# Row sums of squares for the first norm: a second load of x with its sums on ScalarE, in place of GpSimd additions

## The chip, the cores and the metric

One core of a Trainium2 chip runs the whole program. The metric is device time in microseconds (us), median of three runs. Engines: TensorE (PE in the profile; its weight loads are PEld), VectorE (DVE), ScalarE (ACT), GpSimd (POOL), and SyncE (SP), from whose queue nearly all DMA transfers are issued.

## The reference

A hybrid decoder layer on x of 512 tokens by 2048 columns, float32:

```python
h = _rmsnorm(x, norm_w[l])              # x * rsqrt(mean(x*x over the 2048 columns) + 1e-6) * norm_w
p = h @ w_in[l]                         # 2048 x 7824
y_a = _rwkv7_mix(...)                   # RWKV-7 time mixing, 16 heads of 64
y_b = _moba_mix(...)                    # block attention, 4 heads of 128
y_c = _gla_mix(...)                     # gated linear attention, 4 heads of 128
x = x + jnp.concatenate([y_a, y_b, y_c], axis=-1) @ w_out[l]
return _rmsnorm(x, final_norm_w)
```

The norm's factor per token, rsqrt(mean(x*x) + eps), commutes with the product by w_in. The kernel multiplies x by norm_w and by w_in first and applies the factor to the product. So the sums of squares are not needed for the first products, but for whatever reads them.

## The kernel before, in words

**Products.** w_in is computed in 62 jobs of 128 columns, in the order of `ORDER` (lines 40 to 42): wdad, k0, ga0, ga1, r0, k1, low, v0, r1, v1, gk0, gq0 and so on. A job is four units (`low` is a single one of 16 columns); a unit is one load of 128x512 of w_in and its products: four blocks of 128 rows, and for each three matmuls of 128x512, as each operand is split into a float32r high part and the rest (`hhi`, `hlo` for x, `hi`, `lo` for the weights). A unit is thus 12 matmuls. The first three jobs run side by side, since the transposed x arrives only then: units 0 to 11 are wdad, k0, ga0 for the first quarter of x's columns, then for the second, and so on. Units 12 to 15 are ga1, 16 to 19 r0, 20 to 23 k1, 24 low, 25 to 28 v0, 29 to 32 r1, 33 to 36 v1, 37 to 40 gk0, 41 to 44 gq0.

**Buffers.** A unit is loaded into one of three `raw` buffers (the load waits until the split of the unit three before it is done), split by ScalarE (`hi`, line 173) and VectorE (`lo`, line 133) into one of four pairs `hi`, `lo`. So the split of unit u waits for TensorE's last product of unit u-4, and `begin(u)` issues the splits up to unit u+3 ahead of everything else that unit u needs.

**Banks.** A job adds up in one of four PSUM banks `gb`, taken in turn: a job takes the bank of the job four before it and must wait until that one is evacuated (`evac`, line 340: VectorE multiplies it by `rstd_b`, the factor of each token). `job_bank` (line 180) calls `wait_free` for that, and `force` (line 303) then emits whatever work is left up to the evacuation. 62 jobs make 58 such hand-overs.

**Side work** (the mixers) is written as generators that `pump` (line 295) resumes between the products. When, a rough clock model of the queues decides (`Clock`, line 62). The result is a fixed order of instructions on each engine; the engines take their queues strictly in that order.

**The statistics** are such side work: `square` (line 1093) squares each of the 16 transposed tiles of x on ScalarE into `f1` to `f3`, GpSimd adds them into `f0` (line 1103), and `stats` (line 365) sums `f0` over the partitions by four matmuls against a column of ones (line 116), copies the result to `rst`, scales it (line 149), takes the power -1/2 on GpSimd (line 362), spreads it by four transposes (line 125) and copies it to `rstd_b` (line 153). Every evacuation waits for `rstd_b`.

Of the kernel before, what the change touches and what calls it, by code (L numbers as in the profile page):

```python
# [25 lines left out]
# first columns of the parts of w_in  # L26
# [4 lines left out]
# columns of the per-partition parameters  # L31
P_NW, P_MU, P_W0, P_A0, P_KK, P_KA, P_RK, P_LW, P_LB, P_GB, P_GN = 0, 16, 41, 49, 57, 65, 73, 81, 89, 97, 99
NPAR = 100
# columns of the constants
# [4 lines left out]
# the tiles of 128 columns of the input projection, in the order in which they are computed  # L39
# [13 lines left out]
N_FIRST = 3  # L53
# [8 lines left out]
class Clock:  # L62
    """A rough model of the engines' queues, used only to choose the order of emission."""
# [29 lines left out]
def tile_hybrid(ctx: ExitStack, tc: tile.TileContext, x, xT, wu, wlow, wout, par, cst, w2a2_d, aup_d, fw, out):  # L93
# [121 lines left out]
    # RWKV: four heads (two pairs) at a time  # L215
# [23 lines left out]
    # the parts that live where others have been used up  # L239
# [7 lines left out]
    # the lanes of the triangular solves, once the rest of the preparation is over  # L247
# [7 lines left out]
    # the transposed x, before the branches start  # L255
# [3 lines left out]
    fb = [sb(f"f{i}", [128, S]) for i in range(8)]  # L259
    fo = (fb[0], fb[2])  # L260
# [34 lines left out]
    def pump():  # L295
        """Resume the side work whose operands are there by now."""
        for s in list(sides):
            now = ck.t["pe"]
            if runnable(s) and s.ready + MARGIN <= now and ck.t["dve"] < now + BACKLOG and ck.t["act"] < now + BACKLOG:
                resume(s)  # L300
        sides[:] = [s for s in sides if not s.done]

    def force(flag, what):
        """Let the tensor engine wait until the side work has got to flag."""
# [52 lines left out]
    def rsqrt(v, r, scale, e):  # L357
        """r = (v scale + e)^-1/2"""
# [6 lines left out]
    def stats():  # L365
        yield lambda: squares[0] == KT
        ck.cur.start = max(ck.cur.start, ck.t["pool"])
        yield None
        b = yield from bank()
        for tb in range(4):  # L370
            mm(sbk[b][:, tb:tb + 1], fb[0][:, 128 * tb:128 * tb + 128], ones)
        vcopy(rst[:, 4:8], sbk[b][:, 0:4])
        release(b)
# [31 lines left out]
    def resets(t):  # L405
        """1, and 0 where a chunk starts"""
        ck.add("pool", 1.0)
        nc.gpsimd.memset(t, 1.0)
        nc.gpsimd.memset(t[:, 0:S:C], 0.0)
# [3 lines left out]
    def parts(src):  # L413
        """src in two parts that add up to it exactly, each of them float32r"""
# [95 lines left out]
    def a_stage(q, c):  # L510
        """the products within chunks c and c + 1; the two heads of a pair take different row tiles and so banks"""
# [35 lines left out]
    def key_norms(q, j):  # L547
        """the squared norms of the unnormalised keys of a token, laid out as the lanes of solve()"""
# [25 lines left out]
    def solve():  # L574
        """Tt: -(diag(n2) + L)^-1, transposed; one diagonal block of 32 per lane, then the block beside them."""
# [55 lines left out]
    def y_pair(q, cp):  # L631
        """the mix of chunks 2 cp and 2 cp + 1, tokens on the partitions"""
# [23 lines left out]
    def chain(q):  # L656
# [3 lines left out]
        for c in range(NC):  # L660
# [22 lines left out]
            if c < NC - 1:  # L683
# [7 lines left out]
                if c >= 2:  # L691
                    # the state that is overwritten has been read
# [93 lines left out]
    def by_chunks(src, parts):  # L786
        """Transposes src: head h's columns of every chunk of tokens to the half h of the partitions."""
# [13 lines left out]
    def gla(g):  # L801
# [64 lines left out]
        vt = [fb[(4, 7)[i]].rearrange("p (c n) -> p c n", n=128) for i in range(2)]  # chunks 0 to 3, 4 to 7  # L866
# [64 lines left out]
    def moba(h):  # L931
# [5 lines left out]
        def window(w, p, pT):  # L937
            """128 queries: their scores, the softmax over the keys so far, its product with the values"""
# [80 lines left out]
    for g in range(4):  # L1019
# [3 lines left out]
        for n in first[1:]:  # L1023
            add_unit(("in", n, g))
    for n, _ in JOBS[N_FIRST:]:
# [3 lines left out]
        for g in range(4):  # L1029
            add_unit(("in", n, g))  # L1030
    n_in = len(units)
# [14 lines left out]
    late_adds, squares_of = [], []  # L1046
    load_end, split_end = {}, {}
# [3 lines left out]
    # the operands of the last pass take the place of the branches' tiles  # L1051
# [14 lines left out]
    def load(i):  # L1066
        kind, n = items[i]
        dep = 0.0
        if kind == "x":
# [23 lines left out]
    def square(n, r):  # L1093
        """the sum of squares of x"""
        if n == 0:
            act(fb[0], r, AF.Square)
        else:
            e = act(fb[1 + n % 3], r, AF.Square)
            late_adds.append((n, e))
        while late_adds and (len(late_adds) > 2 or n == KT - 1):  # L1100
            m, e = late_adds.pop(0)
            ck.add("pool", 1.25, e + 0.2)
            nc.gpsimd.tensor_tensor(fb[0], fb[0], fb[1 + m % 3], op=ALU.add)  # L1103
            squares[0] = m + 1

    def split(i):
        kind, n = items[i]
        dep = load_end[i]
        if kind == "x":
# [4 lines left out]
            squares_of.append((n, r))  # L1114
# [15 lines left out]
    def advance(u):  # L1130
        """Emit the loads and splits for the units up to u."""
# [3 lines left out]
        while split_done <= last:  # L1135
# [6 lines left out]
            if squares_of and (len(squares_of) > 1 or items[split_done - 1][0] != "x"):  # L1142
                square(*squares_of.pop(0))
# [213 lines left out]
```

## Time and profile before

| what | us |
|---|---|
| median of 3 runs (1071.03 to 1071.57) | 1071.08 |
| span of the profiled execution | 1069.9 |
| TensorE busy in it | 1044.7 |
| VectorE, ScalarE, GpSimd busy | 667.7, 444.6, 71.9 |

The profiled execution is given by its span, from its first to its last instruction; the median stands 1.2 us above it. Read the table by stage: a busy TensorE is one with matmuls in flight, at whatever clock it was granted, and a microsecond in which it waits is a microsecond of the kernel unless something later waits anyway. Matmuls overlap, so the distance from one start to the next is their price, not the duration.

### The profile page before, as it was taken

What the parts mean: (1) busy time and instruction counts of PE and PEld (TensorE: products, weight loads), DVE (VectorE), ACT (ScalarE), POOL (GpSimd) and SP (SyncE); (2) the same over time, 40 slices, a digit from 0 to 9 for tenths busy, and PEclk for the clock granted to TensorE, in tenths of its full rate; (3) what the DMA queues carried; (4) which work ended last, traced back from release to release, by engine and by line L of the source; (5) the groups of instructions that cost most, each with busy time, mean ns of one, the idle gap of its engine ahead of it and who ended that gap; (6) DMA issues with size and microseconds to landing.
All of it is one profiled execution on the core that took longest, in us unless ns stands there. A gap on an engine that the chain in (4) does not pass through costs nothing.

```text
span 1069.9 us, 16750 instructions
## 1 busy us (share of the span) xinstructions
PE 1044.7 (98%) x6376; PEld 819.0 (77%) x6376; DVE 667.7 (62%) x1345; ACT 444.6 (42%) x789; POOL 71.9 (7%) x73
## 2 busy tenths in 40 slices
PE   7799999999999999999999999999999999899996
PEld 5577888767778886777887777788877787688885
DVE  6646669656856885676778665667955564434343
ACT  6464543343454433235534423545322354423333
POOL 4500000000100000000000001000000000102020
PEclk9899999999999999999999999999999999999999
DMA  7232333412233342223334222333341245543434
GB/s 248 94 90 86 89 89 99 108 57 83 80 104 90 100 113 71 70 82 112 94 94 118 66 70 74 85 98 100 105 103 51 80 148 168 177 154 94 164 119 157
DMA packets 80400, 111.87 MB, mean 105 GB/s; under 512 B 28208, under 2 KB 29424, under 8 KB 80192
## 3 DMA queue, kind: packets, MB, share of 16 engines
q1 hardware_dynamic: 80176, 109.76, 34.7%
q8 instruction: 50, 0.82, 0.3%
q0 software_dynamic: 144, 1.05, 0.3%
q14 instruction: 30, 0.25, 0.1%
HBM read 98.62 MB, written 12.16 MB: 104 GB/s over the span
## 4 chain that ended last, share of the span: by engine, by line
PE 89%; DMA 3%; DVE 2%; ACT 2%; issue 2%; POOL 2%; SPq 0%; ACTq 0%; POOLq 0%; DVEq 0%
PE gb L120 67%; PE sb L116 11%; PE sb L120 10%; PE sb L125 2%; POOL f L1103 2%; DVE scr L133 1%; DMA raw<-in_wout_dram 1%; DVE lo L133 1%; DMA raw<-mix 1%; ACT hhi L173 1%; DMA Ld<-Lt 0%; ACT hi L173 0%; DMA raw<-in_wu_dram 0%; ACT f L173 0%; DMA scr<-Ld 0%
## 5 line engine op out<-in xcount | busy, mean ns | idle before, releaser
L120 PE MATMUL gb<-hhi,hi 128*128 128x512 f32 x976 | 404.6, 415 | 6.3 <-ACT hi L173 6.3
L120 PE MATMUL gb<-hhi,lo 128*128 128x512 f32 x976 | 383.7, 393 | 0.8 <-DVE lo L133 0.8
L120 PE MATMUL gb<-hlo,hi 128*128 128x512 f32 x976 | 383.0, 392 | 0.0
L173 ACT ACTIVATE hi<-raw 128x512 fp32r<-128x512 f32 x296 | 186.1, 630 | 398.7 <-PE gb L120 274.7
L133 DVE TENSOR_TENSOR lo<-raw,hi 128x512 fp32r<-128x512 f32 x296 | 213.1, 723 | 213.4 <-ACT hi L173 210.3
L120 PEld LDWEIGHTS gb<-hhi,hi 128*128 128x128 f32 x976 | 184.3, 189 | 51.5 <-ACT hi L173 6.5
L120 PEld LDWEIGHTS gb<-hhi,lo 128*128 128x128 f32 x976 | 184.1, 189 | 42.0 <-DVE lo L133 1.9
L120 PEld LDWEIGHTS gb<-hlo,hi 128*128 128x128 f32 x976 | 184.7, 189 | 33.7 <-issue 1.0
L133 DVE TENSOR_TENSOR scr<-scr 64x30 f32<-64x30 f32 (+14 forms) x240 | 77.5, 323 | 7.2
L120 PE MATMUL gb<-hi,hhi 128*128 128x512 f32 x128 | 50.2, 392 | 2.4 <-ACT hi L173 2.4
L120 PE MATMUL gb<-lo,hhi 128*128 128x512 f32 x128 | 50.2, 392 | 0.4 <-DVE lo L133 0.4
L120 PE MATMUL gb<-hi,hlo 128*128 128x512 f32 x128 | 49.9, 390 | 0.0
L173 ACT ACT_TABLE_LOAD x34 | 43.6, 1283 | 1.0 <-DVE VS L153 0.4
L153 DVE COPY VS<-sb 64x128 f32<-64x128 f32 x64 | 18.5, 288 | 33.5 <-PE sb L116 32.4
L173 ACT ACTIVATE Lt<-sb 64x256 f32<-64x256 f32 (+1 forms) x64 | 19.3, 327 | 33.0 <-PE sb L116 30.4
L362 POOL TENSOR_TENSOR gn<-gn,mhalf 128x16 f32<-128x16 f32 x4 | 12.0, 2995 | 307.1 <-DVE gn L149 307.1
L173 ACT ACTIVATE f<-sb 64x256 f32<-64x256 f32 (+3 forms) x52 | 17.3, 363 | 35.9 <-PE sb L125 19.1
L120 PE MATMUL sb<-lo,hhi 128*128 128x512 f32 x80 | 31.2, 390 | 0.0
L120 PE MATMUL sb<-hi,hlo 128*128 128x512 f32 x80 | 31.2, 390 | 0.0
L120 PE MATMUL sb<-hi,hhi 128*128 128x512 f32 x80 | 31.2, 389 | 0.0
L120 PEld LDWEIGHTS gb<-hi,hhi 128*128 128x128 f32 x128 | 24.0, 188 | 8.1 <-ACT hi L173 3.2
L120 PE MATMUL sb<-late,hhi 128*128 128x512 f32 x96 | 30.0, 394 | 0.0
(229 smaller groups left out, 1145.8 us busy)
## 6 DMA issues: line engine op xcount, KB each, us to landing
raw<-in_wu_dram SPq DMA_DIRECT2D x244, 256.0 KB
raw<-in_wout_dram SPq DMA_DIRECT2D x64, 256.0 KB
raw<-mix SPq DMA_DIRECT2D x16, 256.0 KB
f<-in_x_dram SPq DMA_DIRECT2D x16, 256.0 KB
Ld<-Lt SPq DMA_DIRECT2D x4, 512.0 KB
mix<-f SPq DMA_DIRECT2D x8, 256.0 KB
mix<-ARB SPq DMA_DIRECT2D x8, 256.0 KB
AW<-in_xT_dram SPq DMA_DIRECT2D x6, 256.0 KB
```

Source lines behind the costliest of these rows:

```text
L116: nc.tensor.matmul(o, l, r, start=start, stop=stop)
L120: nc.tensor.matmul(o, l, r, start=start, stop=stop)
L125: nc.tensor.transpose(o, i, ident[:k, :k])
L133: nc.vector.tensor_tensor(o, a, b, op=op)
L153: nc.vector.tensor_copy(o, a)
L173: nc.scalar.activation(o, a, f, **kw)
L362: nc.gpsimd.tensor_tensor(r, v, mhalf[:, 0:n], op=ALU.pow)
L1103: nc.gpsimd.tensor_tensor(fb[0], fb[0], fb[1 + m % 3], op=ALU.add)
```

## The change

x is loaded a second time, as it lies in memory: 128 tokens on the partitions, 2048 columns each. Three blocks of tokens go whole into `BKt`, `VS` and `ARB`, the fourth in four pieces into `f0` to `f3` (all unused at that time). ScalarE squares each in place with a running sum along the row, straight into `rst` (the fourth through `small` and one reduction on VectorE). The 16 squares of the transposed tiles, the 15 GpSimd additions and the four matmuls against ones are gone.

```diff
+    xtok = [[(t, 0)] for t in (BKtf, VSf, ARBf)] + [[(fb[i], S * i) for i in range(4)]]
...
     def stats():
-        yield lambda: squares[0] == KT
-        ck.cur.start = max(ck.cur.start, ck.t["pool"])
-        yield None
-        b = yield from bank()
-        for tb in range(4):
-            mm(sbk[b][:, tb:tb + 1], fb[0][:, 128 * tb:128 * tb + 128], ones)
-        vcopy(rst[:, 4:8], sbk[b][:, 0:4])
-        release(b)
+        yield lambda: squares[0] == 4
+        red(rst[:, 7:8], small[:, 0:4])
         yield None
         yield from rsqrt(rst[:, 4:8], rst[:, 0:4], 1.0 / D, NORM_EPS)
...
+    items.extend(("xt", tb) for tb in range(4))
     for n, _ in JOBS[N_FIRST:]:
...
         for g in range(4):
             add_unit(("in", n, g))
+            if n == JOBS[N_FIRST][0]:
+                items.append(("sq", g))
...
+        if kind == "xt":
+            rows = x[128 * n:128 * n + 128]
+            for o, c in xtok[n]:
+                nc.sync.dma_start(o, rows[:, c:c + numel(o)])
...
-    def square(n, r):
-        if n == 0:
-            act(fb[0], r, AF.Square)
-        else:
-            e = act(fb[1 + n % 3], r, AF.Square)
-            late_adds.append((n, e))
-        while late_adds and (len(late_adds) > 2 or n == KT - 1):
-            m, e = late_adds.pop(0)
-            ck.add("pool", 1.25, e + 0.2)
-            nc.gpsimd.tensor_tensor(fb[0], fb[0], fb[1 + m % 3], op=ALU.add)
-            squares[0] = m + 1
+    def square(tb):
+        for i, (o, _) in enumerate(xtok[tb]):
+            act(o, o, AF.Square, accum=small[:, i:i + 1] if len(xtok[tb]) > 1 else rst[:, 4 + tb:5 + tb], dep=xt_end[tb])
+        squares[0] += 1
```

The seven loads (`xt`) stand on SyncE's queue behind the load of unit 11 and ahead of that of unit 12; the four squares (`sq`) on ScalarE's behind the splits of units 12, 13, 14 and 15. As the clock model sees other times, the order of the side work is written anew as well; three places of it follow.

**TensorE, end of ga1 and start of r0.** `rst` spread by transposes (line 125), ga1 in bank `gb3`, r0 in `gb0`; a piece of the difference, whose last part is that place:

```order
-L116 MATMUL sb0_167<-consts_108,f0_151 128x1 x4
 L120 MATMUL gb0_163<-hhi12_89,hi1_101 128x512
...
-L125 MATMUL sb1_168<-consts_108,rst_118 128x128 x4
 L120 MATMUL gb1_164<-hhi12_89,hi2_102 128x512
...
 L120 MATMUL gb3_166<-hhi15_95,lo3_107 128x512
+L125 MATMUL sb0_167<-consts_108,rst_118 128x128 x4
 L120 MATMUL gb0_163<-hhi0_65,hi0_100 128x512
```

The matmuls against ones stood ahead of unit 9 and the transposes behind it; now the transposes stand behind the last product of unit 15, directly ahead of r0's first.

**VectorE, the statistics and wdad's evacuation.** `lo0` to `lo3` are the split's low parts, of unit u in `lo` number u mod 4. Before (the first row is unit 10):

```order
L133 TENSOR_TENSOR lo2_106<-raw1_98,hi2_102 128x512
L133 TENSOR_TENSOR lo3_107<-raw2_99,hi3_103 128x512
L153 COPY rst_118<-sb0_167 128x4
L133 TENSOR_TENSOR lo0_104<-raw0_97,hi0_100 128x512
L149 TENSOR_SCALAR rst_118<-rst_118 128x4
L133 TENSOR_TENSOR lo1_105<-raw1_98,hi1_101 128x512
L153 COPY rstd_b_116<-sb1_168 128x512
L133 TENSOR_TENSOR pbuf0_139<-gb0_163,rstd_b_116 128x512
```

Of the change (the first row is unit 16):

```order
L133 TENSOR_TENSOR lo0_104<-raw1_98,hi0_100 128x512
L133 TENSOR_TENSOR lo1_105<-raw2_99,hi1_101 128x512
L157 TENSOR_REDUCE rst_118<-small_162 128x1
L133 TENSOR_TENSOR lo2_106<-raw0_97,hi2_102 128x512
L133 TENSOR_TENSOR lo3_107<-raw1_98,hi3_103 128x512
L149 TENSOR_SCALAR rst_118<-rst_118 128x4
L153 COPY rstd_b_116<-sb0_167 128x512
L133 TENSOR_TENSOR pbuf0_139<-gb0_163,rstd_b_116 128x512
```

The evacuation of wdad (last row) stood behind the split of unit 13; now the scaling, the copy and the evacuation stand behind that of unit 19.

**VectorE, v0's evacuation**, whose bank `gb3` gq0 takes at unit 41. Before (the first row is unit 40):

```order
L133 TENSOR_TENSOR lo0_104<-raw1_98,hi0_100 128x512
L139 SCALAR_TENSOR_TENSOR vT_142<-pbuf1_140,params_109,vT_142 128x512
L133 TENSOR_TENSOR AW_125<-vT_142,Pb_141 128x8x64
L139 SCALAR_TENSOR_TENSOR s31_146<-s31_146,params_109,vT_142 128x512
L133 TENSOR_TENSOR lo1_105<-raw2_99,hi1_101 128x512
L133 TENSOR_TENSOR lo2_106<-raw0_97,hi2_102 128x512
L133 TENSOR_TENSOR pbuf0_139<-gb3_166,rstd_b_116 128x512
```

Of the change (the first row is unit 44):

```order
L133 TENSOR_TENSOR lo0_104<-raw2_99,hi0_100 128x512
L133 TENSOR_TENSOR AW_125<-scr_143,Pb_141 128x8x64
L153 COPY PC_136<-Pb_141 128x8
L133 TENSOR_TENSOR pbuf1_140<-gb0_163,rstd_b_116 128x512
L139 SCALAR_TENSOR_TENSOR vT_142<-pbuf1_140,params_109,vT_142 128x512
L564 RECIPROCAL n2l_137<-n2l_137 64x32
L133 TENSOR_TENSOR AW_125<-vT_142,Pb_141 128x8x64
L139 SCALAR_TENSOR_TENSOR s31_146<-s31_146,params_109,vT_142 128x512
L133 TENSOR_TENSOR pbuf0_139<-gb3_166,rstd_b_116 128x512
```

The evacuation of v0 (last row) stood behind the split of unit 42; now it stands eight instructions behind that of unit 44.

## Rows read from the trace of the kernel before

**Rows 1.** The page: the span, and busy time and instructions of each engine.

```profile
span 1069.9 us, 16750 instructions
PE 1044.7 (98%) x6376; PEld 819.0 (77%) x6376; DVE 667.7 (62%) x1345; ACT 444.6 (42%) x789; POOL 71.9 (7%) x73
```

**Rows 2.** What TensorE waited for: total us, times, longest us.

```profile
PE sb L116 <- POOL f L1103: 6.0, 1, 6.0
```

**Rows 3.** TensorE's timeline: start us, us, the instruction, in brackets idle before and releaser.

```profile
8.20 0.29 PEld L120 LDWEIGHTS gb<-hlo,hi 128*128 128x128 f32 x1 [0.50 <-DVE hlo L139]
...
12.27 0.50 PE L120 MATMUL gb<-hhi,lo 128*128 128x512 f32 x1 [0.33 <-DVE lo L133]
...
29.50 0.49 PE L120 MATMUL gb<-hhi,lo 128*128 128x512 f32 x1 [0.46 <-DVE lo L133]
...
34.41 0.39 PE L120 MATMUL gb<-hhi,lo 128*128 128x512 f32 x1
40.76 1.86 PE L116 MATMUL sb<-consts,f 128*128 128x1 f32 x8 [5.96 <-POOL f L1103]
...
48.38 0.47 PE L120 MATMUL gb<-hhi,hi 128*128 128x512 f32 x1
```

**Rows 4.** The chain that ended last, in order of time: start us, us, what.

```profile
42.62 5.33 PE gb L120 x12
47.95 0.67 PE sb L125 x4
48.62 19.05 PE gb L120 x84
```

**Rows 5.** Windows: us; PE, PEld, DVE, ACT, POOL busy; PEclk; DMA share; GB/s.

```profile
35.00:40.00 5.00, 0.00 (x0) 0.00 (x0) 5.00 (x4) 1.98 (x4) 4.76 (x4) 0.81 0.14 54
...
45.00:50.00 5.00, 5.00 (x18) 3.98 (x18) 1.74 (x3) 0.63 (x1) 0.79 (x4) 0.67 0.12 45
...
50.00:250.00 200.00, 200.00 (x1263) 155.60 (x1262) 127.44 (x260) 91.50 (x159) 4.79 (x8) 1.00 0.31 87
...
918.00:922.00 4.00, 2.27 (x9) 1.65 (x10) 1.99 (x3) 1.80 (x3) 0.00 (x0) 1.00 0.34 111
```

**Rows 6.** GpSimd's additions (groups, 0 to 60 us) and a VectorE split during them.

```profile
L1103 POOL TENSOR_TENSOR f<-f,f 128x512 f32<-128x512 f32 x15 | 23.5, 1566 | 7.7 <-ACT f L173 6.7
32.78 1.78 DVE L133 TENSOR_TENSOR lo<-raw,hi 128x512 fp32r<-128x512 f32 x1
```

**Rows 7.** A window of full DMA; ScalarE at a fresh load; its accumulator read.

```profile
24.00:26.00 2.00, 2.00 (x10) 1.67 (x9) 0.21 (x1) 0.29 (x1) 1.77 (x3) 1.00 1.05 398
37.39 0.63 ACT L173 ACTIVATE hi<-raw 128x512 fp32r<-128x512 f32 x1 [0.52 <-DMA raw<-in_wu_dram]
931.82 0.19 ACT L173 ACTIVATION_READ_ACCUMULATOR pbuf<-BK 128x1 f32 x1
```

**Rows 8.** Timelines of ScalarE, VectorE and GpSimd: a split, the statistics' last steps.

```profile
47.56 0.63 ACT L173 ACTIVATE hi<-raw 128x512 fp32r<-128x512 f32 x1 [9.54 <-PE gb L120]
...
43.36 0.16 DVE L149 TENSOR_SCALAR rst<-rst 128x4 f32<-128x4 f32 x1
48.22 0.69 DVE L133 TENSOR_TENSOR lo<-raw,hi 128x512 fp32r<-128x512 f32 x1 [4.71 <-ACT hi L173]
48.83 0.68 DVE L153 COPY rstd_b<-sb 128x512 f32<-128x512 f32 x1
...
43.60 1.03 POOL L362 TENSOR_TENSOR rst<-rst,mhalf 128x4 f32<-128x4 f32 x1 [2.89 <-DVE rst L149]
```

**Rows 9.** Timelines of VectorE and ScalarE: the evacuation of r1 and what follows it.

```profile
130.92 0.69 DVE L133 TENSOR_TENSOR pbuf<-gb,rstd_b 128x512 f32<-128x512 f32 x1
133.71 0.74 DVE L139 SCALAR_TENSOR_TENSOR vT<-pbuf,params,vT 128x512 f32<-128x512 f32 x1
134.48 0.69 DVE L133 TENSOR_TENSOR AW<-vT,Pb 128x512 f32<-128x512 f32 x1
...
131.65 0.72 ACT L173 ACTIVATE vT<-pbuf,omu 128x512 f32<-128x512 f32 x1 [0.71 <-DVE pbuf L133]
```

More of the change, by code (lines that the diff above doesn't have):

```diff
@@ L1045, in tile_hybrid @@
     loaded, split_done = 0, 0
-    late_adds, squares_of = [], []
-    load_end, split_end = {}, {}
+    load_end, split_end, xt_end = {}, {}, {}
     unit_end = {}
@@ L1068, in load @@
         dep = 0.0
+        if kind == "sq":
+            return
+        if kind == "xt":
+            rows = x[128 * n:128 * n + 128]
+            for o, c in xtok[n]:
+                nc.sync.dma_start(o, rows[:, c:c + numel(o)])
+            ck.t["dma"] += 3.0
+            xt_end[n] = ck.t["dma"] + 2.0
+            return
         if kind == "x":
@@ L1091, in load @@
         load_end[i] = ck.t["dma"] + 2.0
-    def square(n, r):
-        if n == 0:
-            act(fb[0], r, AF.Square)
-        else:
-            e = act(fb[1 + n % 3], r, AF.Square)
-            late_adds.append((n, e))
-        while late_adds and (len(late_adds) > 2 or n == KT - 1):
-            m, e = late_adds.pop(0)
-            ck.add("pool", 1.25, e + 0.2)
-            nc.gpsimd.tensor_tensor(fb[0], fb[0], fb[1 + m % 3], op=ALU.add)
-            squares[0] = m + 1
+    def square(tb):
+        for i, (o, _) in enumerate(xtok[tb]):
+            act(o, o, AF.Square, accum=small[:, i:i + 1] if len(xtok[tb]) > 1 else rst[:, 4 + tb:5 + tb], dep=xt_end[tb])
+        squares[0] += 1
     def split(i):
         kind, n = items[i]
+        if kind == "xt":
+            return
+        if kind == "sq":
+            square(n)
+            return
         dep = load_end[i]
@@ L1113, in split @@
                                dep=max(dep, ck.t["act"] + 0.2))
-            squares_of.append((n, r))
             return
@@ L1141, in advance @@
             split_done += 1
-            if squares_of and (len(squares_of) > 1 or items[split_done - 1][0] != "x"):
-                square(*squares_of.pop(0))
         ck.cur = cur
```

## The prediction

> **What bounds the kernel now.** First the page's busy times: TensorE has matmuls in flight for 1044.7 of 1069.9 us, no other engine is near that [rows 1]. A busy engine may be slow, so the windows come next: from 50 to 250 us TensorE does not idle at all and runs at the full granted clock [rows 5], and the chain of waits gives 84 products in 19.05 us from 48.62 on, 0.227 us each, 2.72 us for a unit of 12 [rows 4]. All time there is to win or lose is therefore time in which TensorE waits or runs at its lower level (1.2 instead of 2.4 GHz). The list of its waits names one of size: 6.0 us for GpSimd's additions, in front of the matmuls against ones [rows 2]. The timeline shows the place: the last product of unit 8 starts at 34.41, the next instruction at 40.76 [rows 3]. In that wait the clock falls (mean 0.81 from 35 to 40, and 0.67 from 45 to 50, so it comes back only near the end [rows 5]), and the 12 products of unit 9 take 5.33 us instead of 2.72 [rows 4]. Unit 10 starts at 48.38 [rows 3]. The additions also slow VectorE: a split that takes 0.69 us [rows 8] takes 1.78 while they run [rows 6]. That is why splits come late at 12.27 and 29.50 [rows 3].
>
> **What the change removes.** Unit 9 may follow unit 8 at 34.41 + 0.23 = 34.64. From there to unit 10 before: 48.38 - 34.64 = 13.74 us, of which 2.72 stay: **11.0 us** go. They hold the wait, the matmuls against ones, the transposes (which move) and the lower clock. Ahead of that go the waits for late splits, 0.33 and 0.46 us, and most of the 0.50 us before 8.20, where ScalarE had put a square ahead of the next high part [rows 3]: **1.3 us**, bounds 0.8 and 1.7. Together 12.3 us, bounds 11.8 and 12.7. The end of ga0, before at 48.38 + 24 x 0.227 = 53.8, comes at 41.5, and ga1's, 4 units on, at 52.4. The 23.5 us of additions themselves [rows 6] are worth nothing beyond this, and the 16 squares of 0.6 us give ScalarE air that nobody waits for.
>
> **What it adds: a second load.** Seven transfers of 4.19 MB in all stand on SyncE's queue behind unit 11's load, which waits for the split of unit 8, and that for the end of unit 4, four units before 34.64 and 1.3 us earlier: 34.64 - 10.9 - 1.3 = 22.4, the split done by 24. At the 398 GB/s of a full window [rows 7] they last 10.5 us, to about 35. Unit 12's load, queued behind them, lands near 36 and is split by 37.4; ga1 needs it at 41.5. So I cost the load at nothing, with a cover of 4 us. The Trainium skill (DMA: Bandwidth & Descriptors, Specifications) puts the limit of memory for one core at about 358 GB/s; the row is above it, and by the page the load would take an estimated 11.7 us and the cover would be 2.9. It speaks against the change only through rival 3.
>
> **Squares on ScalarE.** The trace has no row of 2048 columns; four rows of 512 [rows 7] bound it from above, 4 x 0.63 + 0.19 = 2.7 us, the reading of the sum included, and one such row from below, 0.8. With a split's 0.63 that is at most 3.3 us a unit over units 12 to 15, against 2.72 of TensorE: at most 2.4 us lost of the cover. I take no cost; the upper end would delay unit 16's split, and so unit 19's load, by some 0.6 us.
>
> **What it moves: three waits for a bank.** The order matters more than the additions. Units are split four ahead: the split of unit u waits until TensorE has ended unit u-4. If a bank's evacuation stands on VectorE's queue behind the split of unit u+3, then unit u, which needs that bank, cannot start until TensorE has stopped, ScalarE and VectorE have made that split, and the evacuation is through. Of the 58 hand-overs none stands so before (which is why rows 5 show no idle from 50 to 250); in the changed order three do: wdad to r0, k0 to k1, v0 to gq0. Behind the first 1230 or so of TensorE's 4350 instructions in the order the two are the same, so what is lost by then stays lost.
>
> *At r0* (unit 16). After the last product of unit 15: ScalarE's high part to VectorE's low part 0.66 (47.56 to 48.22), to the scaling 0.61, to GpSimd 0.24 (43.36 to 43.60), the power 1.03 [rows 8], four transposes 0.67 [rows 4] and 0.2 to VectorE, the copy 0.7, the evacuation 0.7 [rows 8, 9], and some 0.2 of hops: **5.0 us**. The squares are long done. If unit 19's load, which takes 2.8 us from the end of a split at 34.56 to its use at 37.39 [rows 6, 7], is late because unit 16's split was, it is 6.
>
> *At k1* (unit 20). High part and low part 0.66 + 0.61, evacuation 0.69, hops 0.1 [rows 8]: **2.0 us**, bounds 1.8 and 2.5.
>
> *At gq0* (unit 41). Behind unit 44's split (0.66 + 0.61) come a product into `AW` (0.6), a copy of 8 columns (0.1), r1's evacuation until ScalarE has it (0.73), ScalarE's step (0.78 with the hop), the mix (0.77), the reciprocal (0.3), `AW` again (0.6), one more mix (0.75), and v0's evacuation (0.7) [rows 8, 9]: 6.6 us. Four transposes run inside it and need no time later, 0.4 at the full clock: **6.2 us**, bounds 5.5 and 7.5 (the reciprocal waits for transfers as well).
>
> Sum of the three: 13.2 us, bounds 12.3 and 16. Against 12.3 removed: **+0.9 us** without the clock.
>
> **The clock.** The one long wait of the trace, 6.0 us, brought the fall [rows 3, 5]; a stop of about 2 us at 918 to 922 left the clock at 1.00 [rows 5]. A fall costs about 2.6 us behind the wait: 5.33 instead of 2.72 us for one unit [rows 4]. At k1 I take none. At gq0 the wait is as long as the one that fell, broken only near its start by the transposes; at r0 it is 5.0 us, with the transposes in its midst and no stretch over 2.7 us without work. So I take **one fall, at gq0: 2.6 us**; bounds 0 and 5.2. The Trainium skill (TensorE: Matmul & The Clock Gate, Part 1) says that the monitor of the clock runs freely and is not started by the wait; by that the same wait may bring a fall or not, which is rivals 1 and 2.
>
> **The sum:** 0.9 + 2.6 = +3.5 us on the profiled span of 1069.9 (then 1073.4), and with the 1.2 us that the median stands above it 1074.6.
>
> **Rivals.**
> 1. *The clock holds at all three waits.* Then only +0.9 is left: 1072.0, not slower than a measurement can tell (0.2%, 2.1 us). For it: no wait is quite the one that fell, as both long ones hold transposes. Against: 5.3 us of gq0's are one stretch. It decides at whether that stretch brings a fall. Chance 0.25.
> 2. *It falls at r0 as well.* Another 2.6: 1077.2. For it: the four transposes are little work. Chance 0.22.
> 3. *The second load holds up ga1.* If the seven transfers run below 4.19 MB / 14.6 us = 287 GB/s, unit 12's split comes late and TensorE waits in front of ga1; at half of 398 GB/s it would be 6.5 us more, 1081; midway 1078. Against: the same queue reached 398 [rows 7]. Chance 0.07.
> 4. *gq0 does not wait*, since the mixes in front of v0's evacuation were not needed to stand behind unit 44's split: then neither the 6.2 nor the fall is paid, 1074.6 - 8.8 = 1065.8, faster. Against: the order puts them there, and a queue is worked off in order. Chance 0.06.
>
> My forecast (one fall) has 0.40.
>
> **Numbers.** About 0.2% or 2.1 us is what can be told from no change: faster is below 1068.9, slower above 1073.2. The forecast's own range is 1072.8 to 1076.6 (bounds of the three waits). Range for 8 in 10: from 1070.5 (rival 1 with the lowest bounds) to 1079.0 (rival 2 with the upper bounds, half of rival 3). Slower holds nearly all of the forecast, rivals 2 and 3 and a fifth of rival 1: 0.66. Same is the rest of rival 1 and the lower end of the forecast: 0.26. Faster: rival 4 and a little: 0.08.
>
> **What would show it.** Right: no L1103 or L116 of one column; VectorE's splits at 0.69 us from the start; TensorE without a break from 11 to about 52 us, unit 12 not waiting for a transfer; then three waits, about 5 us before the first products into r0's bank, 2 before k1's, 6 to 7 before gq0's, their releaser VectorE; a granted clock below 1 behind the last. From a quarter of the kernel on, the same timeline as before, shifted. Wrong: a wait for ga1's weights while `BKt`, `VS` and `ARB` are being loaded (rival 3); no idle time at gq0 (rival 4); or waits at places where the two orders don't differ.

## The result, and the profile after

The change made the kernel slower: 1085.73 us median (1085.01 to 1086.96, four runs) against 1071.05 for the kernel before, a ratio of 1.0142 (95% interval 1.0128 to 1.0157). The forecast was 1074.6 with a range of 1070.5 to 1079.0: the direction and the first places were right, the size was too small by 11 us, outside the range. The profiled execution, the fastest of the four, has a span 13.4 us longer than before.

Of the page of the changed kernel, the lines that answer to [rows 1]; GpSimd has lost its additions, TensorE is longer "busy":

```profile
span 1083.3 us, 16709 instructions
PE 1048.1 (97%) x6368; PEld 819.6 (76%) x6368; DVE 657.6 (61%) x1345; ACT 444.4 (41%) x787; POOL 48.3 (4%) x58
```

What TensorE waited for in the changed kernel (total us, times, longest us); it answers to [rows 2]:

```profile
PE gb L120 <- DVE pbuf L133: 9.6, 3, 6.1
PE gb L120 <- ACT hi L173: 8.4, 3, 5.6
PE sb L125 <- POOL rst L364: 4.9, 1, 4.9
PE sb L120 <- DVE xr L133: 2.5, 1, 2.5
```

The one wait of 6.0 us for the additions is gone, and three new lines stand in its place, VectorE's `pbuf`, GpSimd's `rst` and VectorE's `xr` (the 8.4 for ScalarE is the start and the output stage, much as before). TensorE's timeline of the changed kernel shows where, as [rows 3] did before:

```profile
51.71 0.39 PE L120 MATMUL gb<-hhi,lo 128*128 128x512 f32 x1
56.95 1.11 PE L125 MATMUL sb<-consts,rst 128*128 128x128 f32 x4 [4.85 <-POOL rst L364]
59.67 0.77 PE L120 MATMUL gb<-hhi,hi 128*128 128x512 f32 x1 [1.60 <-DVE pbuf L133]
...
72.77 0.39 PE L120 MATMUL gb<-hhi,lo 128*128 128x512 f32 x1
75.06 0.47 PE L120 MATMUL gb<-hhi,hi 128*128 128x512 f32 x1 [1.91 <-DVE pbuf L133]
...
142.76 0.27 PE L125 MATMUL sb<-consts,BK 128*128 128x128 f32 x1
143.44 0.55 PE L125 MATMUL sb<-consts,BK 128*128 128x128 f32 x3 [0.41 <-DVE BK L133]
150.05 0.79 PE L120 MATMUL gb<-hhi,hi 128*128 128x512 f32 x1 [6.06 <-DVE pbuf L133]
...
179.94 0.39 PE L120 MATMUL sb<-xr,sel 128*128 128x512 f32 x1
182.85 0.50 PE L120 MATMUL sb<-xr,sel 128*128 128x512 f32 x1 [2.52 <-DVE xr L133]
```

From the end of the last product (0.23 behind its start) that is 7.7 us at r0, 2.1 at k1, 7.3 at gq0 (four transposes in it) and 2.7 at a place the prediction didn't have: the second half of the product of `xr` with a table of ones, in the value step of the head pair v1, at 183 us. In front of r0 TensorE now runs from 11 to 52 us with no wait above 0.2 us, as forecast.

Windows of the changed kernel, columns as in [rows 5]; the last figures are the granted clock, the DMA share and GB/s:

```profile
50.00:55.00 5.00, 2.10 (x10) 1.40 (x8) 2.04 (x5) 2.63 (x6) 0.00 (x0) 0.95 0.58 180
55.00:60.00 5.00, 1.45 (x5) 1.08 (x6) 2.56 (x5) 0.44 (x1) 2.17 (x5) 0.50 0.27 78
60.00:65.00 5.00, 5.00 (x13) 3.89 (x13) 0.87 (x2) 4.23 (x7) 0.00 (x0) 0.53 0.02 3
...
76.00:78.00 2.00, 2.00 (x10) 1.62 (x10) 0.00 (x0) 0.00 (x0) 0.00 (x0) 1.00 0.44 107
...
148.00:150.00 2.00, 0.00 (x0) 0.00 (x0) 1.99 (x2) 0.00 (x0) 0.86 (x1) 0.50 0.00 0
150.00:152.00 2.00, 1.95 (x5) 1.57 (x6) 0.75 (x1) 0.72 (x1) 0.00 (x0) 0.50 0.00 0
...
184.00:186.00 2.00, 2.00 (x7) 1.57 (x6) 1.83 (x6) 0.63 (x1) 0.00 (x0) 0.54 0.42 132
186.00:188.00 2.00, 2.00 (x7) 1.52 (x7) 2.00 (x5) 0.00 (x0) 0.00 (x0) 0.61 0.24 24
```

A clock of 0.50 is 1.2 GHz. It fell at r0's wait, gq0's and the one at 183 us, three times where one fall was forecast; k1's wait left it at 1.00 (the window from 76 us).

The whole account can be read from when each unit's first product starts in the two timelines. Between rows of this table other products stand at other places in the two orders, so a single step can be off by a us or two; at 16, 48 and 56 both have done the same work but for the matmuls against ones.

| first product of unit | before | changed | difference |
|---|---|---|---|
| 10 | 48.38 | 35.10 | -13.3 |
| 15 (ga1's last) | 62.06 | 49.22 | -12.8 |
| 16 (r0) | 64.78 | 59.67 | -5.1 |
| 40 | 143.22 | 140.03 | -3.2 |
| 41 (gq0) | 146.41 | 150.05 | +3.6 |
| 48 | 169.53 | 178.57 | +9.0 |
| 56 | 194.45 | 207.89 | +13.4 |

By unit 10 the change had won 13.3 us, 1.0 more than forecast. Of this 0.65 is the start of the very first product, 5.63 instead of 6.28; before_filler and sel_later below, whose first loads are those of the kernel before, start at 5.80 and 5.59, so that part is likely scatter and not the change. By unit 56 it had lost 26.7. Up to some 310 us the side products still stand in another order, but nothing more is lost: the span differs by 13.4 as well.

### The profile page after: what moved, and what is told of

Same layout as the page of the kernel before. It is cut to its first block, busy times and chain, and to the rows that moved or that the text cites. A ratio compares the mean times of both kernels' runs of the same rounds, so it can differ in the third digit from the quotient of the medians.

```text
span 1083.3 us, 16709 instructions
## 1 busy us (share of the span) xinstructions
PE 1048.1 (97%) x6368; PEld 819.6 (76%) x6368; DVE 657.6 (61%) x1345; ACT 444.4 (41%) x787; POOL 48.3 (4%) x58
## 4 chain that ended last, share of the span: by engine, by line
PE 88%; DMA 5%; DVE 2%; ACT 2%; issue 1%; SPq 0%; POOL 0%; ACTq 0%; POOLq 0%; DVEq 0%
PE gb L120 65%; PE sb L116 10%; PE sb L120 10%; PE sb L125 2%; DMA raw<-in_wout_dram 2%; DMA VS<-in_x_dram 1%; DMA raw<-mix 1%; DMA raw<-in_wu_dram 1%; ACT hi L173 1%; DVE lo L133 1%; DVE hlo L133 0%; ACT hhi L173 0%; DMA Ld<-Lt 0%; DMA AW<-in_xT_dram 0%; ACT f L173 0%
## 5 line engine op out<-in xcount | busy, mean ns | idle before, releaser
L133 DVE TENSOR_TENSOR lo<-raw,hi 128x512 fp32r<-128x512 f32 x296 | 206.9, 702 | 231.2 <-ACT hi L173 227.0
L120 PEld LDWEIGHTS gb<-lo,hhi 128*128 128x128 f32 x128 | 24.0, 188 | 6.5 <-DVE lo L133 1.6
```

The costliest lines, as they stand in the source:

```text
L120: nc.tensor.matmul(o, l, r, start=start, stop=stop)
L133: nc.vector.tensor_tensor(o, a, b, op=op)
```

## The experiments

Two theories at the start. **A**: the time goes into the order; the statistics now stand later in it, so that evacuations which TensorE needs stand behind other work on VectorE's queue. **B**: the second load and the squares themselves cost it, by occupying the DMA queue and ScalarE. Beside them **C**: a part of the price is the lower clock that each stop brings. Times in the expectations are on the scale of the first measurement (before 1071.05, changed 1085.7). In the experiments' runs the kernel before took 1068.9 to 1069.4, so ratios to it are what compares; the ratio of the change is 1.0142. The trace of the kernel before, with its span of 1069.9 us, is a long one beside that kernel's runs in the experiments, whose median spans were 1067.2 to 1067.7: a lead that is read against it comes out some 2 us larger than the medians have it.

| run | ratio to the kernel before (95%) | span of its profile, us |
|---|---|---|
| small_load | 1.0125 (1.0104 to 1.0145) | 1078.7 |
| short_squares | 1.0104 (1.0089 to 1.0119) | 1079.0 |
| early_load | 1.0056 (1.0039 to 1.0072) | 1072.9 |
| bank_first | 1.0071 (1.0054 to 1.0088) | 1075.0 |
| v0_apart | 1.0144 (1.0127 to 1.0160) | 1085.6 |
| solve_later | 1.0090 (1.0075 to 1.0105) | 1076.1 |
| filler | 1.0105 (1.0079 to 1.0131) | 1077.0 |
| before_filler | 0.9976 (0.9966 to 0.9987) | 1065.2 |
| dense_first | 0.9983 (0.9973 to 0.9992) | 1066.6 |
| all_places | 0.9981 (0.9972 to 0.9991) | 1063.1 |
| early_sums | 0.9895 (0.9878 to 0.9911) | 1057.4 |
| sel_later | 0.9957 (0.9942 to 0.9972) | 1062.2 |

### Load and squares made small, order kept (small_load)

```diff
-                nc.sync.dma_start(o, rows[:, c:c + numel(o)])
+                nc.sync.dma_start(o[:, 0:32], rows[:, c:c + 32])
...
-            act(o, o, AF.Square, accum=...)
+            ck.add("act", (numel(o) - 32) * 0.00084 - 0.1, xt_end[tb])
+            sc, o = 8.0 if len(xtok[tb]) == 1 else 4.0, o[:, 0:32]
+            act(o, o, AF.Square, scale=sc, accum=...)
```

(The line with `ck.add` leaves the clock model's times, and so the order, as they were.)

> The changed kernel with the same order of instructions, but each second load brings only 32 columns, and each square sums only 32 (scaled to the full sum, so the statistics are estimates from 1.6% of x, and the output differs): load and squares are there and cost next to nothing. Theory A (the order of the three hand-overs costs the time, the load only lengthens the first): the wait at r0 shrinks from 7.7 to about 5.0 us, with its clock fall still there, the other places stay; 1085.7 - 2.7 = 1083. Theory B (the load and the squares themselves cost the time): the wait at r0 and its fall go, 7.7 + 2.8 less, 1075.

TensorE's timeline of this run, at r0:

```profile
54.02 1.12 PE L125 MATMUL sb<-consts,rst 128*128 128x128 f32 x4 [2.50 <-POOL rst L364]
56.74 0.76 PE L120 MATMUL gb<-hhi,hi 128*128 128x512 f32 x1 [1.60 <-DVE pbuf L133]
```

With hardly any load or squares TensorE still stops at r0, for 2.50 + 1.12 + 1.60, some 5.4 us with the hops, and the clock still falls; k1 and gq0 stay as they were, and 183 us stays with 3.08 us. Theory B, by which the wait at r0 and its fall go, falls. The 5.4 is the forecast's 5.0 with the four transposes at half clock (1.12 instead of 0.67). The other 2.3 us of the change's 7.7 are the load's and the squares' share.

### The whole load, short squares (short_squares)

The edit is the second hunk above without the first.

> The changed kernel with the whole second load, but with squares that sum only 32 of its columns each, scaled to the full sum (the statistics are estimates from 1.6% of x, and the output differs): the load without ScalarE's time for the squares. With next to no load and no squares the wait at r0 was 5.4 us, 2.3 less than in the change. If ScalarE's squares hold up the splits of units 16 to 19: all of that gain is there, r0 5.4 us and 1083.3. If the load does (unit 12's split at 40.0 and all loads behind it late): r0 stays near 7.7 us and 1085.7.

Unit 12's split is as late as in the change (39.82 against 39.99), held by the load, and yet TensorE waits only 2.50 + 1.06 + 1.60 at r0. So the 2.3 us are the time of the squares, which come late because the load does. ScalarE's timeline of the changed kernel shows how:

```profile
39.99 0.63 ACT L173 ACTIVATE hi<-raw 128x512 fp32r<-128x512 f32 x1 [9.73 <-DMA raw<-in_wu_dram]
40.53 1.90 ACT L173 ACTIVATE BKt<-BKt 128x2048 f32<-128x2048 f32 x1
...
49.62 0.62 ACT L173 ACTIVATE f<-f 128x512 f32<-128x512 f32 x1
50.15 0.18 ACT L173 ACTIVATION_READ_ACCUMULATOR f<-f 128x1 f32 x1
50.24 1.86 ACT L173 ACTIVATE hi<-raw 128x512 fp32r<-128x512 f32 x3
54.26 0.63 ACT L173 ACTIVATE hi<-raw 128x512 fp32r<-128x512 f32 x1 [2.17 <-DMA raw<-in_wu_dram]
```

Everything waits until 39.99 for unit 12's weights, which lie behind the second load on SyncE's queue. Then ScalarE has splits and squares back to back until unit 16's split at 50.24. Unit 19's load needs the buffer that this split frees, so unit 19's split comes at 54.26, and the scaling of the statistics stands behind it on VectorE.

### The load earlier (early_load)

```diff
         for n in first[1:]:
             add_unit(("in", n, g))
+        items.append(("xt", g))
+        if g > 0:
+            items.append(("sq", g - 1))
-    items.extend(("xt", tb) for tb in range(4))
```

(The fourth square follows unit 13.)

> The changed kernel with the four parts of the second load spread over the first 12 units (one behind each group of three) and each squared a group later, so that the statistics are there before unit 16 and wdad's evacuation stands ahead of unit 18's split; the orders at k1 and gq0 are as in the change. Theory A: TensorE does not stop at r0, 7.7 us and a clock fall of about 2.8 less, 1075; the waits at k1 (1.9), gq0 (7.3) and the one at 183 us stay. Rival: the load now competes with the first loads of x and of weights, TensorE waits for weights in the first 40 us, and some us of this are given back: 1078 or more.

As A has it: no stop at r0, no fall there, the three others unchanged (1.92, 6.06 and 2.45 us in its timeline). TensorE did not wait for weights in the first 40 us. The profile's span is 10.4 us shorter than the change's, the ratio 0.9 percentage points lower, some 9 us of the 10.5 expected.

### The old bank before the new splits (bank_first)

```diff
     for u in range(n_in):
+        kind, n, g = units[u]
+        o = job_bank(n)
         begin(u)
...
-        kind, n, g = units[u]
-        o = job_bank(n)
```

> The changed kernel with two steps of the emission swapped: the wait for the old bank's evacuation comes before the splits up to unit u+3, not behind them; the second load is untouched. Theory A: the waits at k1 (1.9) and gq0 (7.3, with a clock fall of about 2.0) go; at r0 the squares are still late, so that about 4.5 of 7.7 us stay; 1085.7 - 1.9 - 9.3 - 3.2 = 1071.3, and about 1067 if the wait at 183 us with its fall also goes. Theory B (the load and the squares): only what they delay can go, and as they are untouched, no more than 2 us: 1084 or above.

A miss by half. k1's wait went. At r0 2.03 + 0.65 + 1.60 us are left, as expected, but at gq0 4.58 us stay, where all should have gone. VectorE's timeline of this run in front of v0's evacuation, the last row:

```profile
138.81 0.69 DVE L133 TENSOR_TENSOR pbuf<-gb,rstd_b 128x512 f32<-128x512 f32 x1
140.29 0.75 DVE L139 SCALAR_TENSOR_TENSOR vT<-pbuf,params,vT 128x512 f32<-128x512 f32 x1 [0.79 <-ACT vT L173]
141.07 0.69 DVE L133 TENSOR_TENSOR AW<-vT,Pb 128x512 f32<-128x512 f32 x1
141.68 0.74 DVE L139 SCALAR_TENSOR_TENSOR s<-s,params,vT 128x512 f32<-128x512 f32 x1
142.35 0.33 DVE L564 RECIPROCAL n2l<-n2l 64x32 f32<-64x32 f32 x1
142.61 0.62 DVE L133 TENSOR_TENSOR pbuf<-gb,rstd_b 128x512 f32<-128x512 f32 x1
```

No split of unit 44 stands in front of it any more. What does is the end of the first pairs' chain (r1's evacuation, its mix, two products), which v0's evacuation is written to follow. From the end of unit 40 to gq0 it is still 5.8 us instead of 7.3, and of the 1.5 that went 1.0 is one mix of 0.74 us that had taken 1.74 in the change. The theory had to be widened: not the split behind which it stands, but the whole chain is late, since it begins with the statistics.

### v0 on its own (v0_apart)

```diff
+    def take_v0():
+        yield from evac("v0", bv[1])
+        flags["v0"] = True
...
+    spawn("v0", take_v0())
```

(`pair_v` then mixes v0 out of `bv[1]`.)

> The changed kernel with one edit: v0's bank is evacuated by a side track of its own into a buffer that is free then (bv1), as soon as v0's products are done, and not at the end of the first pair's decay, key and receptance steps. Load, squares and the hand-overs at r0 and k1 stay. Theory A (at gq0 the evacuation comes late because it hangs at the end of that chain of steps, which starts when the statistics are there): the wait at gq0, 7.3 us, and the clock fall behind it, about 2, go: 1085.7 - 9.3 = 1076.4. The order behind differs, so that places further on (v1's hand-over) may wait in turn; that would be seen there. Rival (TensorE waits at gq0 for something else that is as late, the split of unit 44 or a transfer): 1 to 2 us less, 1084.

gq0's wait went, and yet the kernel is no faster. TensorE stops at the next hand-over of this chain instead, v1's.

```profile
178.47 0.79 PE L120 MATMUL gb<-hhi,hi 128*128 128x512 f32 x1 [5.62 <-DVE pbuf L133]
```

The clock falls there too. That takes back some 5 us of a lead over the change of some 11 (units 48 and 49), and 7.0 are left at unit 56. They are lost between units 140 and 160, from 510 to 580 us, in an order that differs there: TensorE stops for 2.12 us at 537.84 and for 2.04 at 574.43, the second with a fall of the clock. Why it waits there was not followed. A late chain isn't mended at the place where it first shows, and a new order brings waits of its own.

### The wait at 183 us (solve_later)

```diff
     def solve():
+        ck.cur.start = max(ck.cur.start, ck.t["pe"])
         dma(Ld, Lt, nc.sync)
```

> The changed kernel with the model's clock for the triangular solve's trip through memory started when the trip is issued, and not at the end of an earlier step; on VectorE the solve's first step then stands four rows later, behind the parts of the product that TensorE waits for at 183 us. The three hand-overs are as in the change. Theory A (that wait is VectorE's queue blocked for 4.5 us by the solve's wait for its transfer): the 2.5 us and the clock fall behind it (1.7) go, 1081.5; the orders behind it differ, which may move later places by a us. Rival (TensorE waits there because the value chain itself is late): no change, 1085.7.

The wait at 183 us is gone, with its fall. In the changed kernel VectorE's timeline had shown what blocked it:

```profile
175.19 1.22 DVE L133 TENSOR_TENSOR scr<-scr,n2l 64x1024 f32<-64x1024 f32 x1 [4.48 <-DMA scr<-Ld]
...
182.12 0.68 DVE L133 TENSOR_TENSOR xr<-s,xr 128x512 fp32r<-128x512 f32 x1
```

The solve's first step waits 4.48 us for a round trip through memory, with `xr` queued behind it. Before the change the same step waited 2.45 us at 157.5, with other work ahead of it in the queue, and no product of TensorE was near enough to feel it. The gain is somewhat above the 4.2 us expected (ratio 0.5 percentage points lower, with intervals of 0.15 either way); the stop at r0 was 0.9 us shorter in its profile as well (3.97 instead of 4.85 before the transposes).

### Products that keep TensorE going (filler, before_filler)

```diff
+        if n == "r0" and g == 0:
+            filler(20)
         o = job_bank(n)
+        if g == 0 and n in ("r0", "gq0"):
+            filler({"r0": 8, "gq0": 26}[n])
```

(and 11 ahead of the product at 183 us; `filler` issues products of `hT` into a free bank; in before_filler it is `filler(25)` ahead of the four matmuls against ones.)

> The changed kernel with 65 products of constants of hT into a spare bank, which nobody reads, put where TensorE waits: 20 and 8 at r0 (ahead of and behind the four transposes), 26 at gq0 and 11 at the wait at 183 us; at 0.227 us each they fit into the waits. Theory C (part of the loss is the lower clock behind each wait, since TensorE stopped): the granted clock stays at 1.00 at all three places, and about 2.8 + 2.0 + 1.7 us are saved, with half a us on the transposes: 1079. Rival (the clock falls there for another reason, or the products only take time): 1085.7 or above, with the clock falling as before.

> The kernel before the change with 25 products into a spare bank, which nobody reads, where TensorE waits 6.0 us for GpSimd's additions (25 x 0.227 = 5.7 us). Theory C (the lower clock is what the stop brings): the clock stays at 1.00, the twelve products behind it take 2.72 instead of 5.33 us, the matmuls against ones 0.9 instead of 1.7: 1071.05 - 3.4 = 1067.6. Rival (the clock falls there for another reason): 1071 or above.

C holds for the clock: none of the three places has a fall, and some 4 of the 7 us expected are saved. Windows of filler at r0, then of before_filler behind its wait; the clock is 1.00 in all:

```profile
55.00:60.00 5.00, 4.86 (x24) 3.71 (x23) 2.76 (x6) 1.04 (x2) 2.18 (x5) 1.00 0.22 74
60.00:65.00 5.00, 5.00 (x23) 4.14 (x23) 1.39 (x3) 4.44 (x7) 0.00 (x0) 1.00 0.01 3
```

```profile
40.00:42.00 2.00, 1.62 (x10) 1.11 (x8) 2.00 (x3) 0.00 (x0) 1.40 (x1) 1.00 0.00 0
42.00:44.00 2.00, 2.00 (x12) 1.74 (x12) 1.39 (x4) 0.00 (x0) 0.53 (x1) 1.00 0.50 109
```

Counted by the units' starts, filler saves 3.0 us from unit 15 to 17 (0.5 in the transposes, 2.4 in unit 16) and 1.6 from unit 40 to 45. At 183 us it saves nothing: TensorE is 4.5 us earlier there, but VectorE's `xr` only 2.8, and the 11 products and a stop of 1.72 us fill the time. By unit 56 it is 4.4 us ahead of the change. In before_filler the matmuls against ones and unit 9 take 3.2 us less, 3.5 with the four transposes behind them, where 3.4 were expected; the lead at unit 10 is 2.8 us, since the matmuls against ones started 0.7 later than in the kernel before, and it stays 2.8 to at least unit 75.

### Combined versions (dense_first, all_places)

dense_first has the second load behind units 2, 4, 6 and 8, bank_first's swap and solve_later's line:

```diff
+        items.extend(("xt", i) for i in range(4) if len(units) == (3, 5, 7, 9)[i])
+        items.extend(("sq", i) for i in range(4) if len(units) == (6, 8, 10, 12)[i])
```

> The changed kernel with three edits: the four parts of the second load behind units 2, 4, 6 and 8 and their squares three units later; the wait for the old bank ahead of the splits; the solve's trip counted from its issue. By theory A only gq0's hand-over is left, 4.5 to 6 us with a clock fall of about 2: 1085.7 - 7.7 - 2.8 (r0) - 1.9 (k1) - 1.5 (gq0) - 4.2 (183 us) = 1067.6. Rival (the dense load takes transfers away from the first weights): TensorE waits in the first 35 us and some of it is lost again, 1070 or more.

> The three edits of the run with the dense load, bank first and the solve counted from its issue, and v0's own evacuation as well. By theory A no hand-over is left that waits long: that run's 1067.4 less 5.1 us at gq0 and less the fall, about 2: 1060.5, faster than both kernels, and with it the whole of the 12.3 us that the change was seen to remove. If the places further on wait in turn, or the dense load costs transfers elsewhere: 1063 to 1067.

dense_first came out as expected: of the places only gq0's 4.59 us is left (1.30 us for a transfer of a later solve is new, at 401.57), and it is faster than the kernel before by 0.17%. all_places removes gq0's wait as well and has only a 2.60 us stop at v1's hand-over and one of 1.47 us at 521.79. Its lead over the trace of the kernel before is 12.0 us at unit 10, 8.7 at unit 56, where both have done the same work, and 6.8 in the span. Its runs scatter from 1064.9 to 1069.3, the profile is the fastest of the ten, and by the medians it is 2.1 us faster; it missed the 1060.5 by far. Where the rest goes further on, in an order that differs there, was not followed.

### The statistics early, without their cost (early_sums)

```diff
+        if len(units) == 9:
+            items.extend(("sq", i) for i in range(4))
...
-    items.extend(("xt", tb) for tb in range(4))
+        items.append(("xt", g))
...
-                nc.sync.dma_start(o, rows[:, c:c + numel(o)])
+                nc.sync.dma_start(o[:, 0:32], rows[:, c:c + 32])
```

(The squares sum 32 columns as in small_load, this time in the clock model too.)

> The changed kernel with statistics that are there early: of each second load only 32 columns come, spread over the first units, and their squares (scaled to the full sum, so the statistics are estimates from 1.6% of x, and the output differs) stand behind unit 8's split. The transposes of the statistics then stand where they stood before the change, behind unit 9, and no evacuation has to be forced. There are no additions on GpSimd and next to no second load. Theory A (all that the change loses comes from the statistics being there some 7 units later in the order, which makes the first evacuations and the first pair's chain late): none of the waits at r0, k1, gq0 and 183 us is left, and the 12.3 us that were seen to go are won: 1071.05 - 12.3 = 1058.8. Rival (the order behind, or something else that came with the change, costs time by itself): waits stay at these places and the time is 1065 or more.

This is the run that shows the whole. All that TensorE waited for in it:

```profile
PE gb L120 <- ACT hi L173: 8.4, 3, 5.7
PE gb L120 <- DVE lo L133: 0.4, 2, 0.2
PE sb L116 <- ACT f L173: 0.2, 1, 0.2
```

No stop at any of the four places, no fall, and against the trace of the kernel before unit 10 starts 12.0 us earlier (36.33 instead of 48.38) and unit 56 still 12.0 (182.43 instead of 194.45); by the medians it is 11.0. The removed work is worth about what the forecast said (12.3), and the 26 us that the change loses come with statistics that are late in the order. The run can't part the two things in this: with early statistics the clock model also writes TensorE's order, but for four products, as it was before the change. That the order has a share of its own is seen in solve_later, where the wait at 183 us went with the statistics as late as in the change.

### The aim without the second load (sel_later)

In the kernel before, GpSimd sat idle for 7.4 us in the midst of its additions, waiting in its queue for a table of constants that nobody needed yet. Its timeline:

```profile
8.58 8.21 POOL L1103 TENSOR_TENSOR f<-f,f 128x512 f32<-128x512 f32 x5 [6.67 <-ACT f L173]
24.15 0.29 POOL L1198 CAST sel<-consts 128x130 fp32r<-128x130 f32 x1 [7.36 <-DMA consts<-in_cst_dram]
24.40 16.31 POOL L1103 TENSOR_TENSOR f<-f,f 128x512 f32<-128x512 f32 x10
```

```diff
             nc.sync.dma_start(consts, cst)
             load_w2a2(0)
+        if u == 9:
             nc.gpsimd.tensor_copy(sel, consts[:, K_BD:K_BD + 130])
```

> The kernel before the change, with one instruction moved: the copy of two tables of constants (sel) on GpSimd stands behind the fifteen additions, not between the fifth and the sixth, where GpSimd sat idle for 7.4 us until the constants had landed. All orders of the other engines are as before. Theory A's other side (the wait that the change aims at came from this idle time, so it can go without a later statistics chain and without new hand-overs): the additions end at about 33 us, before TensorE needs them; the wait of 6.0 us, the matmuls against ones at half clock (0.9 of 1.7) and the clock fall (2.6) go: 1071.05 - 9.5 = 1061.5, faster than both kernels. Rival (the additions are bound by the squares, which are bound by the load of x): the wait shortens by no more than 2 us, 1068 or more.

TensorE's timeline of this run:

```profile
36.53 1.05 PE L116 MATMUL sb<-consts,f 128*128 128x1 f32 x8 [0.64 <-POOL f L1103]
41.51 0.65 PE L125 MATMUL sb<-consts,rst 128*128 128x128 f32 x4 [1.07 <-POOL rst L362]
```

The 6.0 us are now 0.64, the clock stays at 1.00, and one moved instruction gives the best kernel of the study that computes everything, 0.43% under the one before. It is half of what was expected: the additions end at 36.5, not 33, as they now wait four times for a square of ScalarE (4.0 us in all, by GpSimd's timeline), and units 4 to 8 start 1.1 to 1.9 us later than before (the additions now also run beside VectorE's splits from 17 to 24 us, and TensorE waits 0.63 and 0.72 us for them at 18.59 and 20.27), so that in the trace 6.5 us of 9.5 are left from unit 10 on.

## Why the prediction was wrong

Its terms against what the trace of the change shows. The price of a clock fall is unit 16's time, 59.67 to 64.83, less 2.72 for r0; for the other two it is half of the time in which TensorE worked at 0.50 (150.05 to about 153.4, 184.2 to about 187.6).

| term | forecast, us | measured, us |
|---|---|---|
| removed, by unit 10 | -12.3 | -13.3 |
| units 11 to 14 wait for splits | 0 | 0.5 |
| r0 | 5.0 | 7.7 |
| clock behind r0 | 0 | 2.4 |
| k1 | 2.0 | 2.1 |
| gq0, without its transposes | 6.2 | 6.8 |
| clock behind gq0 | 2.6 | 1.7 |
| at 183 us | none | 2.7 |
| clock behind it | none | 1.7 |
| sum | +3.5 | +12.3 |

The span says +13.4; the other 1.1 us lie in stops and shifts too small to follow singly. The median says +14.7: the profiled execution is the fastest of its four.

- **Right:** what goes, a square of 2048 columns between its bounds (1.90 + 0.18 us), the three hand-overs with their order and releasers, k1, gq0's size, no clock fall at k1, one timeline shifted against the other behind the places where the two orders differ. filler and before_filler bear out the price of a fall.
- **"r0: 5.0 us. The squares are long done"** failed. The mechanism was right (5.4 us in small_load, where the squares are nearly free), but the squares were not done: the last ended at 50.3. Two steps made it so. Unit 12's weights were to land at 36 at 398 GB/s, a rate from one full window [rows 7]; the windows of the change show 238 GB/s from 23 to 26 us, 268 to 29, and 374 to 396 from there to 38, and the split came at 39.99. The cover of 4 us was gone, and ga1 waited for 0.5. And the 2.4 us by which ScalarE was to fall behind were charged against a cover, of which nothing was left by then; the text had both the chain (unit 16's split, unit 19's load) and its effect, at 0.6 to 1 us instead of 2.7.
- **"One fall, at gq0"** failed: three falls, 5.8 us instead of 2.6. Rival 2 had r0's and its chance was 0.22; the argument that the transposes break the stop did not hold: in the change the clock was down before they ran, and in bank_first, where they part r0's wait into 2.03 and 1.60 us, it fell too.
- **The wait at 183 us was not looked for.** The search went through the hand-overs of the four `gb` banks, and compared orders only there. But up to some 310 us (the text's own first 1230 instructions) the side products stand in another order too, and one of those, on a spare bank, waits for VectorE as well. Here solve_later shows the cause, a queue blocked by a transfer.
- **The explanation of gq0** was right in its steps and wrong in its reason. The steps that were added up are the ones that ran, so the size (6.2, measured 6.8) is no luck; the excess is the mix of 1.74 us in place of 0.74, less some smaller steps. But the text had TensorE wait because v0's evacuation stands behind the split of unit 44, and bank_first shows that 5.8 of 7.3 us remain without that split. v0_apart and early_sums show the cause, the chain that begins with the statistics.

With the terms of the missed places (2.7 + 2.4 + 2.7 + 1.7) the same sum would have given 1084.

## What to carry to other kernels

When a change makes a small result available later, follow everyone who needs it, not only the first: the loss comes back at each place where TensorE meets that chain, and taking one such place away moves most of the stop to the next. Compare two orders wherever TensorE waits for another engine, for side products as much as for main ones, and price each stop of some 2 us and more twice, with and without the lower clock. And before replacing slow work, look at why it is late: here the engine that was blamed for its 23.5 us of additions sat idle for 7.4 us in their midst, behind an instruction for somebody else.

## What the runs showed of the hardware

Whether a stop brings a fall isn't told by its length. At about 183 us almost the same stop occurs in several runs: 2.45 us in early_load left the clock at 1.00, 2.52 in the change, 2.66 in bank_first and 2.76 in short_squares brought it down; 2.60 at v1 in all_places did not. In v0_apart 2.12 us at 537.84 left it at 1.00, and 2.04 us at 574.43 brought it down. The windows of early_load, its stop ending at 173.82, then TensorE's timeline and windows of v0_apart:

```profile
170.00:174.00 4.00, 1.55 (x8) 0.96 (x7) 3.76 (x13) 0.63 (x1) 0.00 (x0) 1.00 0.09 31
174.00:178.00 4.00, 4.00 (x18) 3.31 (x19) 3.76 (x11) 0.63 (x1) 0.00 (x0) 1.00 0.39 116
```

```profile
574.43 0.49 PE L116 MATMUL sb<-f,f 128*128 128x128 f32 x2 [2.04 <-DVE f L133]
```

```profile
574.00:576.00 2.00, 1.57 (x6) 1.34 (x7) 1.87 (x5) 0.43 (x1) 0.00 (x0) 0.77 0.49 130
576.00:578.00 2.00, 2.00 (x6) 1.54 (x6) 1.89 (x5) 0.20 (x1) 0.00 (x0) 0.50 0.00 1
```

The Trainium skill (TensorE: Matmul & The Clock Gate, Part 1) says that the monitor runs freely, not started by the work; by that the same stop may or may not bring a fall, and these runs agree. The fall may also come when TensorE is at work again: in the change work resumed at 182.85, and the clock was down from about 184.2 to about 187.6. So the clock's part of an estimate is a range for each stop of this size, not one value. The stop of 1.9 us at k1, in every run that has it, left the clock at 1.00.

VectorE took 1.74 us for a mix of 0.74 [rows 9] at 147.65 in the change, while GpSimd ran an instruction of its own beside it (L566, 1.54 us from 147.31), much as a split was slowed beside the additions [rows 6]. In bank_first that instruction runs from 142.81; the mix, by then done, took 0.74 again, and a split beside it took 1.46. In the change it lay in the midst of gq0's wait, where each microsecond of VectorE is one of TensorE.
